# The last gate stores on another queue, four u tiles between two stages, and denser rows

## The chip, the cores and the metric

The kernel runs on one core of a Trainium2 chip. The core has TensorE (PE), VectorE (DVE), ScalarE (ACT), GpSimd (POOL) and SyncE (SP), each with an instruction queue of its own that is worked off in order; transfers are started from the queues of SP, ACT and POOL. The metric is the device time of one execution in microseconds (us), lower is better. All inputs start in device memory and the output ends there.

## The reference

A decoder block on 1024 tokens of width 1024: RMS norm, one input projection, two gated linear recurrences, an output projection with residual, and then the part that matters here, a feed-forward layer with 16384 experts of one neuron each, followed by a last RMS norm. For each token 8 heads choose 16 experts each (128 in all, with softmax weights g):

```python
act = jax.nn.gelu(jnp.einsum('td,thkd->thk', xb, u[expert]), approximate=False)
return jnp.einsum('thk,thkd->td', (g * act).astype(xb.dtype), v[expert])
```

So every token needs 128 rows of `u` and 128 rows of `v` out of 16384, in float32.

## The kernel before

The 1024 tokens are eight tiles of 128. The projections, the recurrences, the scores and the choice of experts come first, in two halves of four tiles. The expert layer is then computed in two ways side by side.

**Gathered tiles.** For tiles 0 and 1 (and the u part of tile 2) the rows are gathered: GpSimd starts one indirect transfer of 128 rows of 4 KB for each of the 128 choices (L800), and VectorE works on each: a product with a sum for u (L832), a multiply-add into `g_acc` for v (L834). A row is in one of six buffers, and VectorE follows five rows behind the transfers (ROW_LAG). Tile 0 and tile 1 have 128 u rows and 128 v rows each, 512 in all, which run beside the scatter's end and the dense tiles.

**Dense tiles.** For tiles 2 to 7 all 16384 experts are computed on TensorE, as 128 columns j of 128 experts each. For tiles 3 to 7 (640 tokens) the u product of a column ("u tile", `DenseProducts.next`) is two halves of 320 tokens into a PSUM bank `hps`, 8 x 3 matmuls a half, since each float32 operand is split into two parts (`split`, L82 and L83) and three products are added (`mm3`, L93 to L95). The choices become a matrix of gates: `scatter_dense` builds for each tile and each block of 64 tokens a buffer `ot` of [128, 128 columns, 64 tokens] by small matmuls (L921) that ScalarE copies out (L922), and stores it to the array `gd` in eight parts of 16 columns each. Two `ot` buffers alternate.

**Spilled and fresh.** While the gates are not ready, a u tile is spilled: its products are copied to `ht` (L883) and stored to `hd` (L884), 160 KB a half. After the scatter the remaining u tiles are fresh: `fresh` loads the gates of two columns (`gt`, L1001), loads a v tile, and the Gelu (L1008) of each half goes to `ht`, which VectorE multiplies with the gates (L1011). `weigh` splits the v tile and the gates, and `add` multiplies them on TensorE: for three tiles into PSUM sums that stay (`sum`), for three others into `op`, which VectorE adds to `acc` in SBUF (L1050), all once per group of columns. Fresh groups have two columns. When no fresh tile is left, the spilled ones come back (`stored`: L1020, L1023, L1025, Gelu L1026, product L1028), two first, then groups of three (JG). At the end each of the six dense tiles is added up, normed (`final_norm`) and written out.

**The order.** `Weave` is a planner: each piece of work is yielded with planned times (`Work`), it adds these up for each engine and for `span`, and whenever there is room it emits fillers: gathered rows and, during the scatter, dense u tiles. The pace of a row is a planned time of its own: a row can be emitted each time the planned time has grown by PACE, which is PACE[1] (14.0) during the scatter, PACE[2] (2.9) in the fresh stage and PACE[3] (4.2) in the stored stage. `weave.finish(rows)` emits what rows are left at the very end. The planned order is the program's order; the compiler's scheduler may still move an instruction ahead of others on its engine.

After the scatter two u tiles are emitted, and one more if the number done is odd, since fresh groups have two columns. The memory of the scatter's pool (`ot` among it) becomes that of the pool `fresh` (`gt`, `vh`, `vl`, `wh`, `wl`), and a tile in it waits until the old content has been read. Likewise the four PSUM banks `hps` of the scatter stage are given up after the first fresh group. All stores of `gd` are started from ACT's queue: one with each step of the scatter (L954), and the eight of the very last block behind it (L960).

Of the kernel before, what the change touches and what calls it, by code (L numbers as in the profile page):

```python
# [18 lines left out]
P = 128  # L19
# [7 lines left out]
NG = 2  # L27
# [3 lines left out]
TB = 64  # L31
NR = 3
JG = 3
PACE = (2.4, 14.0, 2.9, 4.2)
ROW_BUFS, ROW_LAG = 6, 5

C_HQ, C_HF, C_HI, C_HG = 0, 512, 1024, 1536
C_GQ, C_GK, C_GV, C_GL, C_GG = 2048, 2304, 2560, 3072, 3088
# [540 lines left out]
def query_weights(nc, a, h, pool, load=None, ahead=1):  # L579
    raw = pool.tile([P, KD, 256], F32, name="wq_raw", bufs=ahead)  # L580
    (load or nc.sync.dma_start)(raw, a["peer_w_q"][0, :, h * 256:(h + 1) * 256].rearrange("(k p) n -> p k n", p=P))
    wh = pool.tile([P, KD, 256], F32R, name="wq_h")
    wl = pool.tile([P, KD, 256], F32R, name="wq_l")
    split(nc, wh, wl, raw)
    return wh, wl
# [177 lines left out]
class GatheredTiles:  # L763
# [4 lines left out]
    def __init__(self, weave, tc, a, pool, h_dram, hn_dram, e, g, mixed, tiles, out):  # L768
# [8 lines left out]
        self.act = {c: pool.tile([P, P], F32, name=f"act{c}", bufs=1) for c in [mixed, *tiles]}  # L777
        self.set_pace(PACE[0])

# [125 lines left out]
            self.hold = self.weave.parts  # L905


def scatter_dense(tc, con, wk, ps, e, weights, tiles, gd, nob, lag, before):


    nc = tc.nc
    iota = con["iota"].unsqueeze(1).to_broadcast([P, 4, P])
    steps = TB // 4

    def cols(t, t0):
        return t[:, t0:t0 + 4].unsqueeze(2).to_broadcast([P, 4, P])

    def place(c, tb, t4, ot, oi, oj):
        pt = ps.tile([P, 4, P], F32, name="tp")
        for q in range(4):  # L920
            nc.tensor.matmul(pt[:, q], oi[:, q], oj[:, q], start=True, stop=True)  # L921
        nc.scalar.activation(ot[:, :, t4 * 4:t4 * 4 + 4], pt.rearrange("p t j -> p j t"), AF.Copy)  # L922
        if t4 == steps - 1:
            dst = gd[:, (c - NG) * (P // TB) + tb]
            out.extend((dst[:, q:q + 16], ot[:, q:q + 16]) for q in range(0, P, 16))

    ahead, out = [], []
    for c in tiles:
        before(c)
        ints = wk.tile([P, 2, P], I32, name="ints", bufs=1)  # L930
        nc.vector.tensor_scalar(ints[:, 0], e[:, c], 7, None, OP.arith_shift_right)
        nc.vector.tensor_scalar(ints[:, 1], e[:, c], 127, None, OP.bitwise_and)
        fl = wk.tile([P, 2, P], F32, name="fl", bufs=1)
        nc.vector.tensor_copy(fl, ints)
        tp = ps.tile([P, 4, P], F32, name="tp")
        for q, src in enumerate((fl[:, 0], fl[:, 1], weights[:, c])):
            nc.tensor.transpose(tp[:, q], src, con["ident"])
        sm = wk.tile([P, 3, P], F32, name="sm", bufs=1)
        nc.scalar.activation(sm, tp[:, 0:3], AF.Copy)
        for tb in range(P // TB):  # L940
            ot = wk.tile([P, P, TB], F32, name="ot", bufs=nob)
            for t4 in range(steps):
                t0 = tb * TB + t4 * 4
                oi = wk.tile([P, 4, P], F32, name="oi", bufs=lag + 1)
                nc.vector.tensor_tensor(oi, iota, cols(sm[:, 0], t0), OP.is_equal)
                oj = wk.tile([P, 4, P], F32, name="oj", bufs=lag + 1)
                for q in range(4):
                    t = slice(t0 + q, t0 + q + 1)
                    nc.vector.tensor_scalar(oj[:, q], con["iota"], sm[:, 1, t], sm[:, 2, t], OP.is_equal, OP.mult)  # L949
                ahead.append((c, tb, t4, ot, oi, oj))  # L950
                if len(ahead) == lag:
                    place(*ahead.pop(0))
                if out:
                    nc.scalar.dma_start(*out.pop(0))  # L954
                if c == tiles[-1] and t0 == P - 4:
                    for late in ahead:
                        place(*late)
                yield Work(pe=0.9, dve=1.35, dma=0.7, span=1.7)
    for part in out:
        nc.scalar.dma_start(*part)  # L960
        yield Work(dma=1.5, span=2)


# [16 lines left out]
def experts(tc, a, weave, rows, dense, us, uh, left, right, h_dram, gd, hd, spilled, out):  # L980
# [85 lines left out]
    def head(fp, prep):  # L1066
# [13 lines left out]
        ps = left(pb, "ps_b", 2, space=PSUM, side="right")  # L1080
        rows.set_pace(PACE[3])
        pools[:2] = right(st, "d_g", 2), right(st, "d_va", 2)
# [61 lines left out]
def block_kernel(tc, a, out):  # L1144
    nc = tc.nc
    with ExitStack() as ctx:
# [8 lines left out]
        gd = dram.tile([P, T // TB, P, TB], F32, name="gd")  # L1155
        hd = dram.tile([P, P, NU * P], F32, name="hd")

        def left(stack, name, bufs=1, **kw):
            return stack.enter_context(tc.tile_pool(name=name, bufs=bufs, reuse_waits="tile", **kw))

        def right(stack, name, bufs=1):
            return left(stack, name, bufs, side="right")

        cp = left(ctx, "con")
        con = dict(ident=cp.tile([P, P], F32, name="ident"), iota=cp.tile([P, P], F32, name="iota"))
# [3 lines left out]
        e = rp.tile([P, 8, P], I32, name="e")  # L1169
# [10 lines left out]
        weave, bounds = Weave(), []  # L1180
# [17 lines left out]
        with ExitStack() as c1:  # L1198
# [6 lines left out]
            def first():  # L1205
                for n, w in enumerate(out_proj(tc, a, con["ident"], 0, h_dram, hn_dram, hnT)):
                    yield w
                    if n == 2:
                        wq = query_weights(nc, a, 0, early, paced)
                nc.sync.dma_start(con["iota"], a["c_iota"])  # L1210
                for t, src in zip(hx_d, hnT):
                    nc.sync.dma_start(t, src[:, :, 3 * P:].bitcast(F32))
                sel = Steps(weave, select(tc, left(sx, "sel0", 2), con["iota"], sc_d[0], e[:, 0:4], g[:, 0:4]),
                            Work(dve=6, pool=1), lambda n: n < 4 * scored[0])
                weave.fillers.append(sel)
                for n, w in enumerate(scores(tc, a, hnT, sc_d[0], wq)):
                    scored[0] = (n - 1) // 2
                    yield w
                scored[0] = NH + 1
# [7 lines left out]
        rows = GatheredTiles(weave, tc, a, gpool, h_dram, hn_dram, e, g, NG, range(NG), out)  # L1227
# [10 lines left out]
        dense = DenseProducts(tc, a, right(us, "u", 2), left(uh, "ps_h", 2, space=PSUM, side="right"), hd, hnT)  # L1238
# [5 lines left out]
        dense.ps = left(uh, "ps_h4", 4, space=PSUM, side="right")  # L1244
        rows.set_pace(PACE[1])
        with ExitStack() as c1:
            weave.run(select(tc, left(c1, "sel1", 2), con["iota"], sc_d[1], e[:, 4:], g[:, 4:]))
        with ExitStack() as c1:
            weave.run(scatter_dense(tc, con, left(c1, "sa_wk", 2), left(c1, "sa_ps", 4, space=PSUM),
                                    e, g, [*range(NG + 1, 8), NG], gd, 2, 4,  # L1250
                                    lambda c: rows.finish_mixed() if c == NG else None))

        weave.emit(dense)
        weave.emit(dense)
        while dense.todo[0] % 2:
            weave.emit(dense)
        spilled = dense.todo[0]
        weave.fillers.remove(dense)
        rows.set_pace(PACE[2])
        experts(tc, a, weave, rows, dense, us, uh, left, right, h_dram, gd, hd, spilled, out)  # L1260
# [29 lines left out]
```

## Time and profile before

| | us |
|---|---|
| median of 3 runs | 3434.2 (3431.82 to 3434.51) |
| the profiled execution | 3430.64 |
| its span in the profile | 3428.6 |
| TensorE busy | 3114.4 (91%) |
| VectorE busy | 2604.3 (76%) |
| GpSimd busy | 1087.4 (32%) |
| ScalarE busy | 978.2 (29%) |

A view of the profile gives busy times in stretches of the span, the waits of one engine for another, the instructions of an engine in order of time, or the chain of work that ended last. A row in them names the engine, the line of the kernel, the operation and its output and input by the program's names. `SPq`, `ACTq` mark transfers started from these queues; the time in such a row is that of starting it, not of the transfer. In waits, an instruction's idle time is put down to what ended it. Microseconds are counted from the start of the span. The scatter lies at about 1340 to 1742, the fresh stage at 1742 to 2840, the stored stage up to 3368.

### The profile page before, as it was taken

What the parts mean: (1) busy time and instruction counts of PE and PEld (TensorE: products, weight loads), DVE (VectorE), ACT (ScalarE), POOL (GpSimd) and SP (SyncE); (2) the same over time, 40 slices, a digit from 0 to 9 for tenths busy, and PEclk for the clock granted to TensorE, in tenths of its full rate; (3) what the DMA queues carried; (4) which work ended last, traced back from release to release, by engine and by line L of the source; (5) the groups of instructions that cost most, each with busy time, mean ns of one, the idle gap of its engine ahead of it and who ended that gap; (6) DMA issues with size and microseconds to landing.
All of it is one profiled execution on the core that took longest, in us unless ns stands there. A gap on an engine that the chain in (4) does not pass through costs nothing.

```text
span 3428.6 us, 47839 instructions
## 1 busy us (share of the span) xinstructions
PE 3114.4 (91%) x18146; PEld 2764.0 (81%) x18146; DVE 2604.3 (76%) x5461; ACT 978.2 (29%) x1412; POOL 1087.4 (32%) x894
## 2 busy tenths in 40 slices
PE   8988987889689988999869999999999999999992
PEld 8976777777577988999868888888888888788882
DVE  4266599758675998999777777777777777777777
ACT  4242323233222222444222222222222222333320
POOL 2001134223364332000323444344444443222225
PEclk9999998999899999999989999999999999999996
DMA  5302434344786433555778887888788788888876
GB/s 178 115 16 79 170 130 134 99 149 131 264 322 262 144 112 126 208 198 202 272 260 270 263 269 262 270 259 270 264 274 260 255 265 288 302 269 276 268 230 251
DMA packets 347528, 740.18 MB, mean 216 GB/s; under 512 B 23313, under 2 KB 194722, under 8 KB 347042
## 3 DMA queue, kind: packets, MB, share of 16 engines
q0 software_dynamic: 94464, 343.97, 29.0%
q1 hardware_dynamic: 219426, 313.97, 28.7%
q10 hardware_dynamic: 33408, 79.18, 6.0%
q8 instruction: 142, 2.33, 0.3%
q14 instruction: 88, 0.72, 0.1%
HBM read 635.85 MB, written 101.19 MB: 215 GB/s over the span
## 4 chain that ended last, share of the span: by engine, by line
PE 39%; DVE 16%; DMA 9%; issue 5%; POOL 2%; ACT 1%; ACTq 0%; SPq 0%; DVEq 0%; POOLq 0%
DMA raw<-in_c_u_t 5%; PE op L93 4%; PE hps L93 4%; PE tp L921 4%; PE hps L94 4%; PE op L95 4%; PE hps L95 4%; PE op L94 4%; PE sum L95 3%; PE sum L93 3%; PE sum L94 3%; DVE g_row L832 3%; DVE g_acc L834 2%; DVE ul L83 2%; POOL g_row L800 2%
## 5 line engine op out<-in xcount | busy, mean ns | idle before, releaser
L800 POOL DMA_INDIRECT g_row<-in_c_u_rows,e x384 | 503.2, 1310 | 1012.7 <-DVE g_row L832 871.7
L93 PE MATMUL hps<-hnTh,uh 128*128 128x320 f32 x2048 | 651.3, 318 | 29.4 <-ACT ht L1008 23.8
L95 PE MATMUL hps<-hnTh,ul 128*128 128x320 f32 x2048 | 647.8, 316 | 24.8 <-DVE ul L83 24.8
L94 PE MATMUL hps<-hnTl,uh 128*128 128x320 f32 x2048 | 646.0, 315 | 4.3 <-DVE hnTl L83 4.3
L832 DVE SCALAR_TENSOR_TENSOR g_row<-g_row,g_hn 128x1024 f32<-128x1024 f32 x384 | 464.2, 1228 | 51.9 <-DMA g_row<-in_c_u_rows,e 49.1
L800 POOL DMA_INDIRECT g_row<-in_c_v_rows,e x256 | 318.9, 1246 | 535.6 <-DVE g_acc L834 482.9
L93 PEld LDWEIGHTS hps<-hnTh,uh 128*128 128x128 f32 x2048 | 392.4, 192 | 50.0 <-ACT ht L1008 36.4
L95 PEld LDWEIGHTS hps<-hnTh,ul 128*128 128x128 f32 x2048 | 392.3, 192 | 31.5 <-DVE ul L83 27.4
L94 PEld LDWEIGHTS hps<-hnTl,uh 128*128 128x128 f32 x2048 | 392.3, 192 | 11.0 <-DVE hnTl L83 4.7
L834 DVE SCALAR_TENSOR_TENSOR g_acc<-g_row,g,g_acc 128x1024 f32<-128x1024 f32 x256 | 327.9, 1281 | 12.3 <-DMA g_row<-in_c_v_rows,e 8.0
L93 PE MATMUL op<-vh,wh 128*128 128x512 f32 x768 | 306.5, 399 | 28.9 <-DVE acc L1050 28.6
L1050 DVE TENSOR_TENSOR acc<-op,acc 128x512 f32<-128x512 f32 x330 | 226.4, 687 | 136.1 <-PE op L95 129.3
L95 PE MATMUL op<-vh,wl 128*128 128x512 f32 x768 | 303.0, 395 | 0.0
L94 PE MATMUL op<-vl,wh 128*128 128x512 f32 x768 | 301.8, 393 | 0.0
L95 PE MATMUL sum<-vh,wl 128*128 128x512 f32 x768 | 300.5, 392 | 0.0
L93 PE MATMUL sum<-vh,wh 128*128 128x512 f32 x768 | 299.8, 390 | 0.0
L94 PE MATMUL sum<-vl,wh 128*128 128x512 f32 x768 | 299.8, 390 | 0.0
L83 DVE TENSOR_TENSOR ul<-raw,uh 128x1024 fp32r<-128x1024 f32 x128 | 168.5, 1317 | 140.6 <-ACT uh L82 140.6
L82 ACT ACTIVATE uh<-raw 128x1024 fp32r<-128x1024 f32 x128 | 135.5, 1059 | 412.8 <-PE hps L94 246.2
L921 PE MATMUL tp<-oj,oi 128*128 128x128 f32 x1536 | 211.0, 278 | 4.1 <-DVE oj L949 4.1
L949 DVE TENSOR_SCALAR oj<-iota,sm 128x128 f32<-128x128 f32 x768 | 213.8, 344 | 0.0
L921 PEld LDWEIGHTS tp<-oj,oi 128*128 128x128 f32 x1536 | 195.8, 192 | 8.8 <-issue 5.4
(241 smaller groups left out, 6076.8 us busy)
## 6 DMA issues: line engine op xcount, KB each, us to landing
raw<-in_c_u_t SPq DMA_DIRECT2D x128, 512.0 KB
raw<-in_c_v_rows SPq DMA_DIRECT2D x128, 512.0 KB
gd<-ot ACTq DMA_DIRECT2D x96, 512.0 KB
w_raw<-in_w_in SPq DMA_DIRECT2D x28, 1024.0 KB
gt<-gd SPq DMA_DIRECT2D x37, 768.0 KB
gt<-gd SPq DMA_DIRECT2D x18, 1152.0 KB
hd<-ht ACTq DMA_DIRECT2D x112, 160.0 KB
raw<-hd SPq DMA_DIRECT2D x56, 320.0 KB
```

The lines of the kernel that those rows point to most:

```text
L82: nc.scalar.activation(hi, src, AF.Copy)
L83: return nc.vector.tensor_sub(lo, src, hi.bitcast(F32))
L93: nc.tensor.matmul(out, l[0], r[0], start=start, stop=False)
L94: nc.tensor.matmul(out, l[0], r[1], start=False, stop=False)
L95: nc.tensor.matmul(out, l[1], r[0], start=False, stop=stop)
L800: load = nc.gpsimd.indirect_dma_start(out=row, out_offset=None, in_=self.rows[kind], in_offset=bass.IndirectOffsetOnAxis(ap=self.e[:, c, s ...
L832: nc.vector.scalar_tensor_tensor(row, row, 1.0, self.hn, OP.mult, OP.mult, accum_out=act)
L834: nc.vector.scalar_tensor_tensor(self.acc, row, w, self.acc, OP.mult, OP.add)
L921: nc.tensor.matmul(pt[:, q], oi[:, q], oj[:, q], start=True, stop=True)
L949: nc.vector.tensor_scalar(oj[:, q], con["iota"], sm[:, 1, t], sm[:, 2, t], OP.is_equal, OP.mult)
L1050: last = nc.vector.tensor_add(acc[c][:, ds], op, acc[c][:, ds])
```

## The change

Four things are changed. The eight stores of the last block (L960) are started from SyncE's queue and not from ScalarE's. Their order is turned, so that the block of 16 columns in which the first fresh column will lie comes first and the others follow around the circle; `first` gives that column as the number of u tiles done so far plus EXTRA. Between the scatter and the expert tiles four u tiles are emitted instead of two (and still one more if the number is odd). The paces of the rows beside the expert tiles are 2.75 instead of 2.9 and 3.75 instead of 4.2.

```diff
-PACE = (2.4, 14.0, 2.9, 4.2)
+PACE = (2.4, 14.0, 2.75, 3.75)
 ROW_BUFS, ROW_LAG = 6, 5
+EXTRA = 4
...
-def scatter_dense(tc, con, wk, ps, e, weights, tiles, gd, nob, lag, before):
+def scatter_dense(tc, con, wk, ps, e, weights, tiles, gd, nob, lag, before, first):
...
             dst = gd[:, (c - NG) * (P // TB) + tb]
-            out.extend((dst[:, q:q + 16], ot[:, q:q + 16]) for q in range(0, P, 16))
+            q0 = first() // 16 * 16 if c == tiles[-1] and tb else 0
+            for q in range(q0, q0 + P, 16):
+                out.append((dst[:, q % P:q % P + 16], ot[:, q % P:q % P + 16]))
...
     for part in out:
-        nc.scalar.dma_start(*part)
+        nc.sync.dma_start(*part)
         yield Work(dma=1.5, span=2)
...
                                     e, g, [*range(NG + 1, 8), NG], gd, 2, 4,
-                                    lambda c: rows.finish_mixed() if c == NG else None))
-
-        weave.emit(dense)
-        weave.emit(dense)
+                                    lambda c: rows.finish_mixed() if c == NG else None,
+                                    lambda: dense.todo[0] + EXTRA))
+
+        for _ in range(EXTRA):
+            weave.emit(dense)
         while dense.todo[0] % 2:
             weave.emit(dense)
         spilled = dense.todo[0]
```

## The prediction, made before the result was known

> **What bounds the kernel now.** I read the busy times by stretches first, cutting the part that the change touches at the places where TensorE stops and resumes. Columns: microseconds of the stretch, busy time with instruction count per engine, granted TensorE clock, DMA share, GB/s.
>
> ```profile
> span 3428.6 us, 47839 instructions
> 1692.00:1732.00 40.00, 40.00 (x320) 40.00 (x319) 40.00 (x123) 16.61 (x29) 0.00 (x0) 0.99 0.41 162
> 1732.00:1742.00 10.00, 8.00 (x60) 7.13 (x59) 10.00 (x31) 4.29 (x8) 0.00 (x0) 1.00 0.00 0
> 1742.00:1766.00 24.00, 0.36 (x1) 0.36 (x2) 8.56 (x14) 3.44 (x5) 5.57 (x4) 0.54 0.87 330
> 1766.00:2840.00 1074.00, 1052.35 (x5681) 930.66 (x5681) 817.15 (x1149) 253.33 (x344) 460.08 (x352) 1.00 0.81 267
> 2840.00:3368.00 528.00, 520.36 (x2289) 426.22 (x2287) 412.08 (x450) 154.56 (x190) 143.89 (x128) 0.99 0.81 265
> 3368.00:3428.00 60.00, 0.00 (x0) 0.00 (x0) 44.26 (x37) 2.30 (x4) 37.20 (x32) 0.54 0.83 303
> ```
>
> The two long expert stretches (1766 to 3368) are TensorE's: it is idle for 21.7 and 7.6 us of them. Two stretches are not: 24 us between the scatter and the expert tiles, where it stands still while the DMA engines are full, and 60 us at the end, after its last matmul, where VectorE and GpSimd finish gathered rows. The change aims at both.
>
> For the first gap I read the waits of that neighbourhood, then the instructions of ScalarE, VectorE and SyncE in order of time.
>
> ```profile
> PE hps L93 <- ACT ht L1008: 23.8, 1, 23.8
> DVE vl L83 <- DMA gd<-ot: 15.3, 1, 15.3
> ```
> ```profile
> 1742.47 0.33 SPq L1004 DMA_DIRECT2D raw<-in_c_v_rows  x1
> 1752.78 0.38 SPq L1001 DMA_DIRECT2D gt<-gd  x1
> 1763.61 0.33 SPq L858 DMA_DIRECT2D raw<-in_c_u_t  x1
> 1742.51 8.43 ACTq L960 DMA_DIRECT2D gd<-ot  x8
> 1762.26 1.06 ACT L82 ACTIVATE vh<-raw 128x1024 fp32r<-128x1024 f32 x1 [10.21 <-DMA gd<-ot]
> 1765.15 0.44 ACT L1008 ACTIVATE ht<-hps 128x320 f32<-128x320 f32 x1 [1.84 <-DVE gt L1011]
> 1762.36 2.36 DVE L83 TENSOR_TENSOR vl<-raw,vh 128x1024 fp32r<-128x1024 f32 x2 [15.34 <-DMA gd<-ot]
> 1764.64 1.48 DVE L1011 TENSOR_TENSOR gt<-ht,gt 128x320 f32<-128x320 f32 x3
> ```
>
> Read backwards: TensorE resumes at 1765.6 because a PSUM bank was emptied by the Gelu (L1008), which waited for one of the two `ht` buffers, which waited for the gate product (L1011), which stands on VectorE behind `vl`, whose buffer lies where the scatter's `ot` was and is free when the eight last stores have landed, at about 1762. Before that point TensorE had done all it could: the first two fresh u tiles fill `ht` and four banks.
>
> For the end I read VectorE's and TensorE's last instructions, and how many of the 256 v rows (L834) come after the last dense norm.
>
> ```profile
> 3367.21 0.39 PE L95 MATMUL op<-vh,wl 128*128 128x512 f32 x1
> 3372.47 1.28 DVE L1140 SCALAR_TENSOR_TENSOR raw<-acc,f_rs,nf 128x1024 f32<-128x1024 f32 x1 [1.39 <-POOL f_rs L73]
> 3374.05 1.28 DVE L834 SCALAR_TENSOR_TENSOR g_acc<-g_row,g,g_acc 128x1024 f32<-128x1024 f32 x1 [0.30 <-DMA g_row<-in_c_v_rows,e]
> 3420.07 1.28 DVE L834 SCALAR_TENSOR_TENSOR g_acc<-g_row,g,g_acc 128x1024 f32<-128x1024 f32 x1 [1.22 <-DMA g_row<-in_c_v_rows,e]
> 3374.00:3428.00 54.00, 38.54 (x30) 0.50 0.83 308
> ```
>
> The last line is the stretches view for L834 alone. TensorE ends at 3367.6, the dense tiles' last norm at 3373.8, and then 30 rows run alone, from 3374.05 to 3421.35: 47.3 / 30 = 1.58 us each. The end lies 61.0 us behind TensorE.
>
> **Four u tiles instead of two.** The spilled u tiles are counted by the stores of `ht`:
>
> ```profile
> hd<-ht ACTq DMA_DIRECT2D x112, 160.0 KB
> ```
>
> Two halves a tile: 56 spilled, 72 fresh. After the scatter the planner takes two tiles and one more if the number is odd; with four it comes to 58 spilled and 70 fresh, whichever parity the two had. No matmul is added or dropped; the products of two tiles move from the fresh stage, which TensorE fills, to the gap, which it doesn't. Spilled tiles need no gates, so they run while the stores travel. Their price, from the chain that ended last, 14 such matmuls from 2203.16 to 2205.21 (first and last):
>
> ```profile
> 2203.16 0.15 PE hps L94
> 2205.07 0.15 PE hps L95
> ```
>
> 2.05 / 14 = 0.147 us; a tile is 2 halves x 8 x 3 = 48, so two are 96 x 0.147 = 14.1 us. What they need is there: weights load while DMA is at 0.00 (1732 to 1742), and their splits (VectorE 1.23 us each) fit behind the scatter, where VectorE is busy 8.56 of 24 us. They cost two more stores and loads of `hd` (2 x 2 x 320 KB) and two more ScalarE Gelus in the last stage, where ScalarE is busy 155 of 528 us: nothing on the path. If that cover were gone, TensorE would show it as waits for `wh`.
>
> **Stores on SyncE, block 48 first.** The stores' bytes do not change. The queues' table over the gap (packets, MB, share):
>
> ```profile
> q10 hardware_dynamic: 1152, 4.19, 30.8%
> q1 hardware_dynamic: 1984, 2.36, 21.4%
> q0 software_dynamic: 576, 2.10, 15.1%
> ```
>
> Up to 1762 there moved the stores' 4.19 MB, four rows' 2.10, one v tile 0.52 and the first `gt` 0.79: 7.6 MB from about 1743.3, 18.7 us, 407 GB/s. The gap is a transfer at full rate, and a column order can't shorten it, because `vl` waits for all eight stores and not for the first. `gt` can be asked for earlier (it is issued at 1752.78 now), but not used earlier. What SyncE's queue now does behind the stores counts against the change: eight issues took ScalarE 8.43 us, so a v load, `gt` and a u load that stand behind them on SyncE start up to 8 us later, and of these the u tile and the v tile were already in SBUF before: 8.12 MB at 407 GB/s end at 1763.3, and a second v tile 1.3 us after that. ScalarE is freed of 8.43 us that nobody waits for. Bounds of this part: 4 us earlier (the stores no longer share with `gt`, and the first bank comes free at once) to 8 us later (the whole issue time lands on the path); nearest is the sum of bytes, so I take 2 us later. Gap: 14.1 - 2 = **12 us gained**, bounds 6 and 22 (the gap closed, with the half-clock start).
>
> The Trainium skill, "DMA: Bandwidth & Descriptors", section "Issuing engines are not separate DMA queues", says that transfers started from any engine share the same 16 DMA engines and that another engine only saves issue time; the 0.87 share and 330 GB/s of the gap agree. By it the queue move alone is worth nothing, and the sum above has it so.
>
> **Denser rows.** A row is emitted each time the planner's time has grown by the pace. The planner's times stand in the code: two fresh tiles 14.2 and six additions of 2.7 make 30.4; a group of three stored tiles has six additions of 4.0, so 24.0. Before: 36 x 30.4 = 1094 / 2.9 = 377 rows, then (16.2 + 18 x 24.0) = 448 / 4.2 = 107: 484. VectorE did
>
> ```profile
> 1766.00:3374.00 1608.00, 289.40 (x226) 1.00 0.81 266
> 1766.00:3374.00 1608.00, 303.76 (x504) 1.00 0.81 266
> ```
>
> 226 v rows and 504 / 2 = 252 u rows up to 3374 (the second has a read-out beside each), 478, plus the 5 that lag: 483. So the planner's count can be used. After: 35 x 30.4 = 1064 / 2.75 = 387, then (16.2 + 432 + 16.2) = 464 / 3.75 = 124: 511, 27 more, and 1 more at the old pace beside the two moved tiles. Of 30 rows at the end about 2 are left: 28 x 1.58 = 44 us. Given back: the last group has two tiles instead of three, so the last additions are 72 matmuls of 0.23 us and not 108, 16.7 us and not 25, while VectorE still has six chunks of two additions and a norm there; the last norm falls about 5 us later behind TensorE. **End: 39 us gained**, bounds 25 (ten rows still left) and 50 (TensorE's end, the last norm and a store).
>
> What the rows cost inside the stages: VectorE gets 27 x 1.28 = 35 us more in 1602, from 77% to 79%. Waits of TensorE for it are there already, more with v rows than with u rows:
>
> ```profile
> 2120.00:2300.00 180.00, 177.40 (x962) 156.63 (x960) 135.88 (x212) 42.49 (x59) 77.74 (x61) 1.00 0.81 267
> 2660.00:2840.00 180.00, 172.39 (x936) 152.61 (x935) 139.20 (x148) 40.16 (x54) 81.76 (x61) 1.00 0.81 267
> PE op L93 <- DVE acc L1050: 11.3, 9, 2.5
> ```
>
> 2.6 us of 180 idle with u rows, 7.6 with v rows (the wait is that of 2550 to 2840). I take 10% of the 29 us, **3 us lost**; bounds 0 and 38 (1602 x 7.6 / 180 = 67 instead of 29).
>
> **Sum.** 12 + 39 - 3 = 48 us. The profiled execution took 3430.6 us (span 3428.6), so 3383 by its own scale; the median shown, 3434.2, lies 3.6 higher. I say 3384.
>
> **The rivals.**
> 1. *The gap stays as long.* The first loads of the expert tiles wait behind the stores on SyncE's queue, and TensorE has its 14 us but stands still as long after them. For: the queue is in order and eight issues took 8.43 us; the DMA engines are full there. Against: u tiles that TensorE needs first are asked for before the stores are ready. Gain 36: 3396. The Trainium skill's same page, section "Two DMAs through the same engine are not ordered", says that within a queue descriptors start in order, which is this mechanism; no run here yet shows loads behind these stores.
> 2. *Rows crowd the stages.* VectorE's additions come late behind rows everywhere as they do from 2660 to 2840, 38 us lost instead of 3: gain 13, 3419. Half of it gives 3401. Against: VectorE has a fifth of the time free.
> 3. *Slower.* The same place, the additions of `op` behind rows on VectorE, decides from TensorE's idle share in the two stages: with the gains of 51 us, at (29 + 51) / 1602 = 5% the change is worth nothing; at 6% idle it is 96 us, 67 lost, 3447. The worst stretch now shows 4.2%, so this needs all of both stages worse than the worst now.
> 4. *The rows do not move.* The planner's other limits hold them back and 25 still stand at the end: gain about 10, 3421. Against: 484 planned and 483 seen.
>
> **How the numbers follow.** Forecast 64% (3362 to 3394, about 3384), rival 1 15%, rival 2 11% (3395 to 3424), rival 3 5%, rival 4 5%. The range takes the forecast, rival 1 and half of rival 2: 3362 to 3406. A change of 0.2% (7 us) is what a measurement can tell. Faster 0.92, same 0.03, slower 0.05.
>
> **What would show it.** 116 stores of `hd`; the eight last stores on SyncE, `gt` asked for before 1752; TensorE's gap at about 12 us instead of 23.8. That the clock of 0.54 in the gap persists would agree with the Trainium skill, "TensorE: Matmul & The Clock Gate", Part 1, which has the clock halved after an idle window of some 3.4 us. At the end few L834 behind the last dense norm, and the end 20 to 25 us behind TensorE instead of 61. The prediction is wrong if TensorE's idle time from 1766 on is far above 29 us, or if a gap as long as before stands behind the two tiles.

## The result, and the profile after

The changed kernel takes 3401.4 us (median of 4 runs, 3386.8 to 3403.5), the kernel before 3433.0 us beside it: a ratio of 0.9902, 95% interval 0.9883 to 0.9921, or 32 us less. In a second series it was 3399.1 us (3396.9 to 3406.6), ratio 0.9905 (0.9886 to 0.9923). The profiled execution of the first series is its fastest run, 3386.8 us (span 3384.8); the second series left another profile, of 3397.3 us (span 3395.5). Both are read below. One execution further down, of `six_alternate` (3842.5 us at a granted clock of 0.74), is left out of its ratio.

The lines of the kernel have moved by 1 to 4: the Gelu of a fresh half is L1012, the gate product L1015, `vl` L84, the eight stores L964, the v load L1008, the u load L859, `gt` L1005, the multiply-add of a v row L835, an addition to `acc` L1054, the last norm L1144.

Busy time by stretches, cut where the scatter ends, where TensorE resumes, at the last fresh u product and at the last matmul. First two rows of the kernel before in this cut, then the changed kernel.

```profile
1766.00:2872.00 1106.00, 1084.35 (x5855) 959.13 (x5855) 840.24 (x1174) 259.54 (x353) 472.90 (x362) 1.00 0.81 266
2872.00:3368.00 496.00, 488.36 (x2115) 397.75 (x2113) 388.99 (x425) 148.35 (x181) 131.07 (x118) 0.99 0.81 266
```
```profile
1737.00:1762.00 25.00, 13.17 (x88) 12.91 (x89) 9.60 (x15) 4.04 (x7) 5.58 (x4) 0.83 0.94 345
1762.00:2837.00 1075.00, 1053.85 (x5689) 933.27 (x5690) 837.10 (x1167) 253.02 (x344) 482.46 (x371) 1.00 0.83 276
2837.00:3362.00 525.00, 507.78 (x2184) 409.47 (x2183) 416.93 (x451) 151.34 (x185) 152.86 (x132) 0.99 0.82 272
3362.00:3384.00 22.00, 0.00 (x1) 0.00 (x0) 12.70 (x15) 3.45 (x6) 6.99 (x7) 0.56 0.67 238
```

In the gap TensorE now works 13.2 of 25 us. The fresh stage is 31 us shorter and the stored stage 29 us longer (two u tiles have changed sides, and rows have been added to both), and the stretch behind the last matmul has gone from 60 to 22 us. TensorE's idle time from its resumption to its last matmul is 38.4 us (21.2 + 17.2), where it was 29.3.

TensorE's waits in that time, then the gap in order of time on SyncE, ScalarE and VectorE:

```profile
PE op L94 <- DVE acc L1054: 34.5, 37, 3.6
PE hps L94 <- ACT ht L1012: 12.6, 2, 11.3
```
```profile
1737.59 6.57 SPq L964 DMA_DIRECT2D gd<-ot  x8
1744.26 1.25 SPq L1008 DMA_DIRECT2D raw<-in_c_v_rows  x1
1745.61 1.21 SPq L859 DMA_DIRECT2D raw<-in_c_u_t  x1
1746.86 1.25 SPq L1005 DMA_DIRECT2D gt<-gd  x1
1756.99 1.06 ACT L83 ACTIVATE vh<-raw 128x1024 fp32r<-128x1024 f32 x1 [12.22 <-DMA raw<-in_c_v_rows]
1758.08 1.23 DVE L84 TENSOR_TENSOR vl<-raw,vh 128x1024 fp32r<-128x1024 f32 x1 [14.84 <-DMA raw<-in_c_u_t]
1760.90 0.89 DVE L1015 TENSOR_TENSOR gt<-ht,gt 128x320 f32<-128x320 f32 x2 [0.17 <-DMA gt<-gd]
1761.51 0.44 ACT L1012 ACTIVATE ht<-hps 128x320 f32<-128x320 f32 x1 [2.04 <-DVE gt L1015]
```

The longest wait is halved, 11.3 us where it was 23.8. Three loads that are started behind the eight stores on SyncE's queue (6.57 us) now end it one after the other: the v tile, which is split from 1757.0 on, 12.7 us after its load was started; the u tile right behind it; and the gates, for which the product at 1760.9 waits last (0.17 us). The row of `vl` names the u load, but `vl` starts when `vh` is done (1758.05). The gates are asked for at 1746.9, 9.3 us after the scatter's end (10.3 before). From the scatter's last copy (1737.6) to TensorE's resumption (1762.0) it takes 24.4 us, where it took 23.1.

The end, TensorE's last matmul and then VectorE's and SyncE's last instructions:

```profile
3361.61 0.39 PE L96 MATMUL op<-vh,wl 128*128 128x512 f32 x1
3375.43 1.28 DVE L1144 SCALAR_TENSOR_TENSOR raw<-acc,f_rs,nf 128x1024 f32<-128x1024 f32 x1
3376.62 1.28 DVE L835 SCALAR_TENSOR_TENSOR g_acc<-g_row,g,g_acc 128x1024 f32<-128x1024 f32 x1
3379.93 1.28 DVE L1144 SCALAR_TENSOR_TENSOR g_hn<-g_acc,f_rs,g_row 128x1024 f32<-128x1024 f32 x1 [0.66 <-POOL f_rs L74]
3381.24 0.33 SPq L1145 DMA_DIRECT2D out_dram<-g_hn  x1
```

One row is left behind the last dense norm, where 30 were.

### The profile page after: what moved, and what is told of

Same layout as the page of the kernel before. It is cut to its first block, busy times and chain, and to the rows that moved or that the text cites. A ratio compares the mean times of both kernels' runs of the same rounds, so it can differ in the third digit from the quotient of the medians.

```text
span 3384.8 us, 47850 instructions
## 1 busy us (share of the span) xinstructions
PE 3116.0 (92%) x18146; PEld 2763.2 (82%) x18146; DVE 2598.8 (77%) x5459; ACT 977.3 (29%) x1414; POOL 1083.7 (32%) x894
## 3 DMA queue, kind: packets, MB, share of 16 engines
q0 software_dynamic: 94464, 343.97, 29.3%
## 4 chain that ended last, share of the span: by engine, by line
PE 34%; DVE 18%; DMA 12%; issue 5%; POOL 2%; ACT 2%; SPq 0%; ACTq 0%; DVEq 0%; POOLq 0%
DMA raw<-in_c_u_t 5%; PE hps L94 4%; PE tp L923 4%; PE hps L95 4%; PE hps L96 4%; PE op L94 4%; PE op L96 3%; PE op L95 3%; DVE g_acc L835 3%; DVE g_row L833 2%; DMA raw<-hd 2%; PE sum L94 2%; PE sum L96 2%; DVE ul L84 2%; PE sum L95 2%
## 5 line engine op out<-in xcount | busy, mean ns | idle before, releaser
L94 PE MATMUL hps<-hnTh,uh 128*128 128x320 f32 x2048 | 650.3, 318 | 17.0 <-ACT ht L1012 12.6
L94 PEld LDWEIGHTS hps<-hnTh,uh 128*128 128x128 f32 x2048 | 391.8, 191 | 37.4 <-ACT ht L1012 25.3
L835 DVE SCALAR_TENSOR_TENSOR g_acc<-g_row,g,g_acc 128x1024 f32<-128x1024 f32 x256 | 327.7, 1280 | 8.2 <-DMA g_row<-in_c_v_rows,e 4.0
L1054 DVE TENSOR_TENSOR acc<-op,acc 128x512 f32<-128x512 f32 x330 | 225.6, 686 | 116.2 <-PE op L96 108.0
L84 DVE TENSOR_TENSOR ul<-raw,uh 128x1024 fp32r<-128x1024 f32 x128 | 168.1, 1314 | 145.2 <-ACT uh L83 145.2
L83 ACT ACTIVATE uh<-raw 128x1024 fp32r<-128x1024 f32 x128 | 135.5, 1059 | 409.3 <-PE hps L95 201.2
L94 PEld LDWEIGHTS op<-vh,wh 128*128 128x128 f32 x768 | 144.9, 189 | 78.3 <-DVE acc L1054 50.8
```

What stands on the lines that cost most here:

```text
L83: nc.scalar.activation(hi, src, AF.Copy)
L84: return nc.vector.tensor_sub(lo, src, hi.bitcast(F32))
L94: nc.tensor.matmul(out, l[0], r[0], start=start, stop=False)
L835: nc.vector.scalar_tensor_tensor(self.acc, row, w, self.acc, OP.mult, OP.add)
L1054: last = nc.vector.tensor_add(acc[c][:, ds], op, acc[c][:, ds])
```

## The experiments

All kernels were timed in turn with the kernel before, and each left a profile, in which I measured four pieces: from the scatter's last copy to TensorE's resumption, the fresh stage to the last u product, the stored stage to the last matmul, and the rest of the span. The sum leaves out what lies ahead of the scatter's end, which no kernel here changes. The pieces are those of the one profiled execution, which can lie some 10 us from the median beside it (3398.2 us for `early_rows`, 3424.4 for `queue_only`).

| kernel | to resumption | fresh | stored | end | sum | median us | ratio to before (95%) |
|---|---|---|---|---|---|---|---|
| before | 23.1 | 1106.4 | 495.6 | 61.0 | 1686 | 3433 | 1 |
| changed, first profile | 24.4 | 1074.7 | 525.3 | 22.8 | 1647 | 3401 | 0.9902 (0.9883 to 0.9921) |
| changed, `again` | 24.8 | 1082.0 | 523.7 | 22.3 | 1653 | 3399 | 0.9905 (0.9886 to 0.9923) |
| `extra_only` | 24.8 | 1074.9 | 515.4 | 78.6 | 1694 | 3432 | 0.9993 (0.9976 to 1.001) |
| `pace_only` | 23.2 | 1109.8 | 507.2 | 9.0 | 1649 | 3392 | 0.9876 (0.9856 to 0.9896) |
| `queue_only` | 22.8 | 1107.1 | 492.6 | 63.0 | 1686 | 3434 | 1.0004 (0.999 to 1.0018) |
| `no_queue_move` | 24.7 | 1077.0 | 523.3 | 22.2 | 1647 | 3396 | 0.9903 (0.988 to 0.9926) |
| `late_rows` | 25.3 | 1073.4 | 548.2 | 32.3 | 1679 | 3421 | 0.9957 (0.994 to 0.9975) |
| `early_rows` | 25.0 | 1089.7 | 513.4 | 19.0 | 1647 | 3388 | 0.9863 (0.9841 to 0.9886) |
| `early_two` | 22.8 | 1129.2 | 496.2 | 19.5 | 1668 | 3408 | 0.9915 (0.9898 to 0.9932) |
| `no_stored_rows` | 24.7 | 1080.6 | 507.6 | 211.0 | 1824 | 3563 | 1.0381 (1.0363 to 1.0399) |
| `alternate` | 24.7 | 1084.9 | 534.9 | 22.3 | 1667 | 3408 | 0.9927 (0.9908 to 0.9945) |
| `six_tiles` | 18.5 | 1071.6 | 530.0 | 20.9 | 1641 | 3386 | 0.9851 (0.9833 to 0.9869) |

**The same kernel again.** No edit.

> The changed kernel once more. Its first execution took 3386.8 us and three others 3400 to 3403. Theory A (the expert stages differ from run to run): a profile of a run near 3402 shows the same gap (TensorE idle about 12 us) and the same end (about 23 us behind TensorE), but more than 39 us of TensorE idle between the gap and the last matmul. Theory B (the difference lies ahead of the change): the scatter ends some 5 us later than at 1737 and the rest is as before. Theory C (the end differs): rows stand behind the last dense norm again.

The second profile is 10.5 us longer than the first. The scatter ends 5.1 us later (1742.7 and 1737.6), the two stages take 5.7 us more (TensorE idles about 40 us in them), the end is the same. A and B hold by half each, C does not. A single profile of this kernel is thus good to some 10 us, half of it from work that the change doesn't touch.

**Four tiles alone.**

```diff
-        weave.emit(dense)
-        weave.emit(dense)
+        for _ in range(4):
+            weave.emit(dense)
```

> Four u tiles alone; stores, their order and paces as before. Theory plan (what the planner counts comes to pass): 14 us of TensorE's products move into the gap, but the fresh stage is two tiles shorter and so 6.6 rows fewer are emitted at the old paces (1064/2.9 + 464/4.2 = 477.5 against 484), 1 is emitted beside the two tiles, and the last group is shorter: -14 + 9 + 5 = 0, time 3433 within 5. Rival (the end does not depend on it): the 14 us are seen, 3419.

Stretches from TensorE's resumption on (fresh stage, stored stage, end) and the wait in the gap:

```profile
1769.00:2844.00 1075.00, 1055.33 (x5689) 933.43 (x5690) 814.90 (x1148) 253.41 (x344) 457.13 (x352) 1.00 0.81 266
2844.00:3359.00 515.00, 504.97 (x2184) 409.29 (x2182) 403.54 (x439) 152.78 (x185) 140.93 (x120) 1.00 0.79 264
3359.00:3437.00 78.00, 0.00 (x0) 0.00 (x0) 53.91 (x46) 3.45 (x6) 50.21 (x40) 0.52 0.82 289
```
```profile
PE hps L93 <- ACT ht L1008: 12.4, 2, 11.6
```

The plan's theory holds. TensorE gets its time: the two stages take 1590.3 us, not 1602.0, and it has its last matmul 10.0 us earlier after the scatter's end (11.7 less 1.7 that the gap ends later). The end gives it all back, 78.6 us behind TensorE, not 61.0. Two things add up to this. Rows are emitted by planned time, and the plan is 30 us shorter in the fresh stage and 16 us longer in the stored one: 35 rows instead of 30 stand behind the last dense norm. And this norm ends later itself, 11.2 us behind TensorE's last matmul (3359.0) and not 6.2:

```profile
3368.88 1.28 DVE L1140 SCALAR_TENSOR_TENSOR raw<-acc,f_rs,nf 128x1024 f32<-128x1024 f32 x1 [0.45 <-POOL f_rs L73]
```

That is 5.0 us of the 17.6; the other 12.6 are the rows behind it. In the profiles with two u tiles the last dense norm ends 5 to 6 us behind the last matmul, with four (a last group of two stored tiles instead of three) 11 to 16, with six (a last group of one) 17 to 18. That the short last group is the cause fits the expectation; no run here varies it alone. Ratio 0.9993: half of the gap is gone and nothing is won.

**The paces alone.** `PACE = (2.4, 14.0, 2.75, 3.75)` in the kernel before.

> The denser paces alone; two u tiles and stores as before. Theory plan with the crowding seen: 1094/2.75 + 448/3.75 = 517 rows, so none of 512 is left, the end falls from 61 to about 18 us behind TensorE (-43), TensorE waits 10 us more for VectorE's additions: 3400. Rival small crowding (3 us): 3393. Rival heavy crowding (half of the rows' gain given back inside the stages): 3411 to 3415.

```profile
1762.00:2872.00 1110.00, 1085.92 (x5858) 960.41 (x5858) 859.89 (x1193) 260.17 (x356) 491.43 (x381) 1.00 0.83 274
2872.00:3379.00 507.00, 491.41 (x2112) 396.54 (x2110) 405.63 (x439) 147.49 (x181) 148.75 (x128) 0.99 0.82 273
3379.00:3387.00 8.00, 0.00 (x0) 0.00 (x0) 2.73 (x4) 1.15 (x2) 0.55 (x1) 0.79 0.33 131
```

The end falls further than I had it, to 9.0 us, since all rows are done before the last matmul; the stages lose more, 15.0 us (1617.0 against 1602.0), 11.6 of them in the stored one. About 10 of the 15 are idle time of TensorE (24.1 + 15.6 us in these two stretches, 29.3 before), about what was expected. The time, 3391.7 us, is that of the small-crowding rival, but by two larger sizes that balance. It is at least as fast as the whole change: 0.9876 and 0.9905, with intervals that meet. The denser rows are the whole gain. The four tiles add nothing to it: with them the stages are 11 to 17 us shorter and the end 13 to 14 us longer, of which 9 to 10 lie ahead of the last dense norm (14.7 and 14.3 us behind the last matmul, here 5.1).

**The stores alone.** The changed kernel with `EXTRA = 2` and the old paces.

> The eight stores on SyncE's queue with the needed block first, alone; two u tiles and old paces. Theory bytes (the gap is a transfer at full rate): 3433 within 4, TensorE's gap within 3 us of 23.8. Rival first block: the gates come earlier and the gap shortens by 5 us or more, 3428. Rival queue: loads wait behind the stores and the gap grows by 5 to 8 us, 3439.

```profile
PE hps L94 <- ACT ht L1012: 23.5, 1, 23.5
```

The bytes theory holds: the gap is as it was, the ratio 1.0004.

**The change without the stores.** `extra_only` with the new paces.

> The change without its stores: four u tiles and the denser paces, the eight stores on ScalarE's queue in their old order. Theory bytes: the stores' queue and order are worth nothing, 3400 within 4, gap 12 us. Rival: SyncE's queue delays the first loads, so this is 4 us or more faster; or the needed block first helps, so this is 4 us or more slower.

0.9903 beside 0.9902 and 0.9905, the four pieces those of the change. Queue and order of the stores are worth nothing here either. TensorE resumes 24.7 us after the scatter, as late as with the stores on SyncE's queue (24.4 and 24.8), though the wait passes through other landings: the stores', for which `vl` waits as in the kernel before, and then the gates'.

```profile
1762.14 1.23 DVE L83 TENSOR_TENSOR vl<-raw,vh 128x1024 fp32r<-128x1024 f32 x1 [9.88 <-DMA gd<-ot]
1764.00 0.89 DVE L1011 TENSOR_TENSOR gt<-ht,gt 128x320 f32<-128x320 f32 x2 [0.64 <-DMA gt<-gd]
```

So the 1.3 to 1.7 us by which the gap ends later come with the four tiles and not with the queue: `queue_only`, with two tiles, has 22.8. With four, one more u load (0.52 MB) is started just behind the scatter; at the 407 GB/s of the gap before that is 1.3 us, an estimate.

**Where the rows cost.** Two kernels move rows between the stages, one takes them out of the stored stage; all three have the change's four tiles.

```diff
-PACE = (2.4, 14.0, 2.75, 3.75)
+PACE = (2.4, 14.0, 2.9, 3.3)      (late_rows)
+PACE = (2.4, 14.0, 2.64, 4.2)     (early_rows)
+PACE = (2.4, 14.0, 2.75, 1e6)     (no_stored_rows)
```

> The changed kernel with paces 2.9 and 3.3: 1064/2.9 + 464/3.3 = 508 rows, 17 of them moved from the fresh stage to the stored one. Theory stored: the stored stage grows by 15 us or more against the changed kernel, in waits of TensorE for VectorE's additions, time 3415 to 3420. Rival any row: 3400 to 3405 (four rows more at the end).

> The changed kernel with paces 2.64 and 4.2 instead of 2.75 and 3.75: 1064/2.64 + 464/4.2 = 514 rows, as many as the change has, but 16 of them moved from the stored stage to the fresh one. Theory stored (a denser row costs TensorE most in the stored stage): the two stages together shrink from about 1603 us to about 1597, the end stays at 20 us behind TensorE, time 3392. Rival any row (a row costs the same wherever it is): 3400, no change. Rival fresh (the u loads of the fresh stage come late): its part grows by more than 12 us, 3406.

> The changed kernel with no rows emitted in the stored stage (its pace 1000000): all that are left then run at the end. Theory rows cost TensorE time: the stored stage falls from 524 us to 500 to 510 and its waits for VectorE's additions to under 3 us; some 125 rows at 1.4 to 1.6 us each stand at the end, 3560 to 3590 in all. Rival: the additions are late without rows too, the stored stage stays at 520 or more.

The stored stage of each in two views. The stretches view for L835 alone gives the stretch, its length, and VectorE's busy time with v rows with their number in brackets; the waits view gives TensorE's wait for VectorE's additions (sum, number, longest).

`no_stored_rows`, stretches and then waits:

```profile
2846.00:3354.00 508.00, 12.78 (x10) 1.00 0.48 154
```
```profile
PE op L94 <- DVE acc L1054: 3.8, 3, 2.6
```

`early_rows`, stretches and then waits:

```profile
2864.00:3377.00 513.00, 155.30 (x122) 1.00 0.81 266
```
```profile
PE op L94 <- DVE acc L1054: 7.7, 7, 3.0
```

`again`, stretches and then waits:

```profile
2849.00:3373.00 524.00, 169.00 (x132) 1.00 0.81 273
```
```profile
PE op L94 <- DVE acc L1054: 14.9, 15, 3.6
```

`late_rows`, stretches and then waits:

```profile
2841.00:3389.00 548.00, 189.65 (x148) 0.97 0.82 277
```
```profile
PE op L94 <- DVE acc L1054: 29.3, 17, 4.2
```

Read the number of rows against the stage: 10 rows 507.6 us, 122 rows 513.4, 132 rows 523.7, 148 rows 548.2. `extra_only`, also with four tiles, fits in: 118 rows, 515.4. Three profiles with the change's paces give 525.3, 523.7 and 523.3, so the steps beyond 122 rows are clear of this spread. The first 112 rows cost 5.8 us, 0.05 each; the next 10 cost 10.3, 1.0 each; the next 16 cost 24.5, 1.5 each. In the last of these steps only a part is waiting. These are the whole rows of the stretches for `again` and `late_rows` (TensorE's busy time stands first behind the length):

```profile
2849.00:3373.00 524.00, 507.55 (x2190) 409.75 (x2189) 416.69 (x452) 151.31 (x185) 154.00 (x132) 1.00 0.81 273
2841.00:3389.00 548.00, 517.52 (x2184) 416.65 (x2182) 435.34 (x466) 151.97 (x185) 188.36 (x148) 0.97 0.82 277
```

TensorE's waits for the additions grow by 14.4 us, and its busy time for the same work by 10.0, at a granted clock of 0.97 instead of 1.00. That the waits are what lowers the clock is not shown.

A row at the end costs about the same as these last: in `no_stored_rows`

```profile
3354.00:3564.00 210.00, 0.00 (x0) 0.00 (x0) 169.80 (x136) 3.45 (x6) 155.32 (x131) 0.51 0.91 332
```

127 of the 131 instructions of GpSimd are rows, and the last of them is done on VectorE 204 us behind the last matmul: 1.6 us each, with DMA at 0.91. So a row is nearly free up to about 120 in this stage (one in 4.2 us), and beyond that it costs about what it would at the end. Theory stored holds against any row for `late_rows` (3421.0, a microsecond above what was expected); `early_rows` is 0.9863, lower than the change's 0.9905 with intervals that just meet, but its profile shows an exchange and no clear gain: the stored stage 10 us shorter than in `again`, the fresh stage 8 us longer, both together 1603.1 us and not the expected 1597. The fresh stage seems to have such a bend too, with four tiles 1073.4 and 1074.9 us at pace 2.9, 1074.7 to 1082.0 at 2.75, 1089.7 at 2.64; it rests on one profile.

What stands ahead of a late addition can be seen in `pace_only`, on VectorE and TensorE in one group of the stored stage:

```profile
3035.23 5.24 DVE L834 SCALAR_TENSOR_TENSOR g_acc<-g_row,g,g_acc 128x1024 f32<-128x1024 f32 x4
3040.39 1.28 DVE L1050 TENSOR_TENSOR acc<-op,acc 128x512 f32<-128x512 f32 x2
3041.13 0.50 PE L93 MATMUL op<-vh,wh 128*128 128x512 f32 x1 [1.06 <-DVE acc L1050]
```

Four rows in a clump, two additions behind them at once, and TensorE waits 1.06 us for the first. Seven of the ten such waits in this stage have a clump of four just ahead. But the same clump stands in the group before (3009.07 to 3014.31), and TensorE does not wait there. I took the clumps for the cause and spread the additions:

**Alternating order of the additions.**

```diff
+ORDER = (0, 3, 1, 4, 2, 5)
...
-                yield add(old, c)
+                yield add(old, ORDER[c])
```

> The changed kernel with the six tiles of a group added in the order 0, 3, 1, 4, 2, 5, so that the ones whose products VectorE must add up stand between those that stay in PSUM. Theory clump (VectorE works on rows in clumps while the first three tiles are added, and then its additions come late in a row): TensorE's waits for the additions fall from 36 us to under 15, the stored stage from 524 to about 510, time 3383 to 3388. Rival load (VectorE simply has too much to do beside denser rows): waits stay above 30 us, time 3400.

The theory falls in this form: TensorE's waits for the additions from the scatter on grow from 36.2 to 49.0 us, the stored stage to 534.9, the time to 3408. That such clumps stood ahead of late additions is seen; that clumps as such are the cause is not shown, and what makes the additions late stays open. It was tried on `six_tiles` as well:

> The kernel of six_tiles (3385.6) with the same alternating order. Theory clump: waits under 15 us instead of 39, time 3366 to 3372. Rival load: 3386. If the end takes back what the stages gain, the end grows from 21 to over 30 us behind TensorE and the time stays at 3380.

0.9868 (0.9843 to 0.9893) against 0.9851: nothing gained, where 3366 to 3372 us was expected of the clump theory. Only the time speaks here, TensorE's waits were not compared.

**Two tiles with rows moved ahead.** `PACE = (2.4, 14.0, 2.7, 4.2)` in the kernel before.

> The kernel before with paces 2.7 and 4.2 only (two u tiles, stores as before): 1094/2.7 + 448/4.2 = 512 rows. Theory stored: gap 23 us as before, the two stages 1607 us instead of the 1617 with the change's paces, the end 9 to 15 us behind TensorE: 3386. Rival any row: as pace_only, 3392. If four tiles are worth what the gap showed once the rows keep up, this stands 6 to 10 us above early_rows; if not, level with it or below.

A miss by 21 us: 3407.5 (the profiled execution, 3415.1, is the longest of six). The end is at 19.5 us, where 9 to 15 was expected, the stored stage as before, but the fresh stage grew by 22.8 us, much more than in `pace_only` (3.4) at nearly the same pace. Its stretch and TensorE's waits in it, then the waits of the kernel before:

```profile
1768.00:2898.00 1130.00, 1091.99 (x5858) 965.75 (x5859) 873.34 (x1204) 261.01 (x356) 508.85 (x391) 0.99 0.82 274
PE op L93 <- DVE acc L1050: 32.2, 28, 2.5
PE hps L93 <- ACT ht L1008: 28.7, 2, 23.4
```
```profile
PE op L93 <- DVE acc L1050: 21.4, 24, 2.5
```

The waits for VectorE's additions are 10.8 us longer, a Gelu is waited for once more (5.3 us; the other 23.4 are the gap's), and TensorE's busy time is 7.6 us longer (1092.0 against 1084.4) at a lower granted clock. Why 2.7 does this and 2.75 does not, I can't say.

With nearly the same paces as here (2.64 in the fresh stage) four tiles are 20 us better than two (0.9863 and 0.9915), with the change's own paces they are not. By the pieces the stages are 22 us shorter in the one case and the ends alike, in the other they are 11 to 17 us shorter and the end takes that back. What decides between the two is not shown.

**Six tiles.** `EXTRA = 6` and `PACE = (2.4, 14.0, 2.59, 4.2)`.

> Six u tiles between the stages, paces 2.59 and 4.2 so that rows still come out at 513. Theory gap (what is left of the gap is TensorE time to be had as long as the rows keep up): the gap of about 11.5 us closes, the two stages shrink by 12 more, end at 20 us: 3381. Rival loads (the first loads of the expert tiles, behind the stores and later asked for, keep a gap of 8 us or more): 3390. Rival rows (the end takes back what the gap gives): as early_rows, 3392.

```profile
1760.91 0.64 PE L94 MATMUL hps<-hnTh,uh 128*128 128x320 f32 x1 [5.30 <-ACT uh L83]
```
```profile
1761.00:2833.00 1072.00, 1039.98 (x5618) 921.94 (x5619) 847.52 (x1176) 251.47 (x343) 498.04 (x385) 0.99 0.84 282
2833.00:3363.00 530.00, 521.53 (x2256) 424.02 (x2254) 418.74 (x454) 154.24 (x186) 145.22 (x124) 0.99 0.81 267
```

The gap is down to 5.3 us, and the split of a u tile on ScalarE (L83) ends it now; what that split waited for is not clear from the trace. TensorE resumes 6.5 us earlier than in `early_rows` (18.5 against 25.0), but the two stages shrink by 1.5 us only (1601.6 against 1603.1) and not by 12. The fresh stage has 68 tiles; at the 15.4 us a tile of the kernel before (1106.4 / 72) they would take 1045 us, and with 385 rows beside them they take 1072. The time, 3385.6 us, lies between the first two expectations; 0.9851 (0.9833 to 0.9869) is the lowest of all and clear of the change's two ratios, though not of those of `pace_only` and `early_rows`.

## Why the prediction was right, and what was mis-sized

The time came out 17 us above the forecast of 3384: inside the whole range (3362 to 3406), but beyond the part of it that was the forecast's own (up to 3394) and in the part taken in from rival 2. The path was right, rows moved from the end into the stages by denser paces; one term was too small. Step by step:

- **The two u tiles.** 14.1 us moved, the gap's end 2 us later, 12 gained. `extra_only` shows 11.7 less in the stages and 1.7 later: 10.0. Right, except that the 2 us were booked on the stores' new queue and come with the tiles. That TensorE's time would come back at the end was in the count of rows and in the shorter last group, and it did: 17.6 us in `extra_only`.
- **The stores.** Nothing, said the sum of bytes, and `queue_only` and `no_queue_move` say so. The reading of the gap was incomplete, though. I had the eight stores' landing end it; with the stores ahead of them on SyncE's queue it is the first loads, the mechanism of rival 1, for the u tiles that ran in the gap had been loaded before, as was said against it, but the next u load (1745.61) stands behind the stores. It cost nothing, 24.4 and 24.8 us to TensorE's resumption against 24.7 in `no_queue_move`.
- **The clock.** In the remaining gap the granted clock is 0.83 over the stretch, with TensorE at work in half of it, and the first matmul behind it takes 0.64 us, twice the usual 0.31. The Trainium skill's rule in "TensorE: Matmul & The Clock Gate", Part 1, that an idle window of some 3.4 us halves the clock, agrees in kind; in the trace of the changed kernel the half clock begins at 1753.5, 2.8 us after the last matmul, and lasts until 1767.1, 5.1 us after the next one.
- **The end.** 39 us gained, said the count of rows by planned time; 38.2 and 38.7 were measured (61.0 to 22.8 and 22.3). That both agree so closely is luck in part: the last dense norm moved by 8.5 us (from 6.2 to 14.7 behind TensorE) and not by 5, and the rows gave some 47 and not 44.
- **Rows inside the stages.** This is the step that was mis-sized: "I take 10% of the 29 us, 3 us lost". The changed kernel's two stages take 1600.0 and 1605.7 us against 1590.3 in `extra_only`, 10 to 15 us lost; `pace_only` against the kernel before gives 15.0. The argument was VectorE's mean share, 79% with a fifth free. The runs show that the price of a row is not even: 0.05 us up to 122 rows in the stored stage, 1 to 1.5 us beyond. It is rival 2, of which "half of it gives 3401"; that the measured 3401.4 is this very figure is luck, since the other terms were off too.

With that term 10 to 15 us instead of 3, the sum is 34 to 39 us (10 + 38.5 less 10 to 15), against 32 and 33 measured in the medians. The rest is within what two executions of one kernel differ by.

Rival 3 had the same place and did not decide: TensorE's idle share in the stages came to 38.4 / 1600 = 2.4%, not 5%. Rival 4 is refuted by the end.

## What to carry to other kernels

An idle stretch of the busiest engine was worth nothing to fill here as long as the end hung on other work; where a second stream is emitted by the first one's progress, shortening the first leaves more of the second for the end. A filler's price should be measured as a curve (take it out, then raise it in steps): here it is nearly nothing up to a point and then about as much as doing the work alone, and the mean share of an engine shows neither. And one trace against one trace is not enough for 10 us.

## What was not expected of the hardware

Executions of one kernel spread more than the first three had shown: 23 runs of the kernel before lie between 3420.8 and 3451.7 us. In the profiles of the table the scatter, which no kernel here touches ahead of its last stores, ends between 1737 and 1749 us. Eight stores of 512 KB started in a row take their queue 6.6 to 8.4 us, on SyncE as on ScalarE, while a lone one takes 0.33; a load behind them on the same queue came 12.7 us after its own start, with the DMA engines' share at 0.94 over that stretch.
